# One gated recurrence on one core: products of a level in four PSUM banks at once, chunk states as one chain in tiles of their own

## The chip, the core and the metric

The kernel runs on one core of a Trainium2 chip. A core has a matrix engine (TensorE; PE in the profile, PEld for its weight loads), a vector engine (DVE), a scalar engine (ACT), GpSimd (POOL), a sync engine (SP) that issues DMAs, an on-chip memory with 128 partitions (SBUF) and an accumulator memory for matrix products (PSUM), which the kernel uses as eight banks of 128 x 512 f32. The metric is the device time of one execution in microseconds (us). The kernel before took 2295.3 us, the median of three runs.

## What is computed

One layer of a decoder trunk with 1024 tokens and width 1024: a modulated input, one wide input projection, an HGRN2 gated recurrence (8 heads, 128 x 128 states) beside a retention branch (4 heads), a gated merge, an output projection, a layer norm, and a squared-ReLU MLP. All of it is f32. The change lies in the HGRN2 branch alone. Cut to what matters, for each head:

```python
q = silu(zq);  f = lb + (1 - lb) * sigmoid(zf);  k = (1 - lb) * sigmoid(-zf)
# S_t = diag(f_t) S_{t-1} + k_t^T v_t ,   o_t = q_t S_t      (f_t: one factor per channel)
def step(state, blk):                      # one chunk of tokens
    qc, lfc, kc, vc = blk
    b = cumsum(lfc)                        # log of the running product of f
    scores = einsum('id,ijd,jd->ij', qc, exp(b_i - b_j) where i >= j, kc)
    o = scores @ vc + (qc * exp(b)) @ state
    state = exp(b_last) * state + (kc * exp(b_last - b))^T @ vc
    return state, o
o = o * rsqrt(mean(o*o) + eps) * silu(g)   # per head
```

## The kernel before

**The stage.** `build` runs the eight heads in a loop (lines 1711 to 1715). Each head has two parts, which are Python generators that emit instructions: `h_dense(h)` (line 730), the projections of `q`, `f` and `k` for one head, and `h_rec(p, hd)` (line 770), its recurrence. `weave` (line 89) alternates the emission of `h_dense(h + 1)`, four steps, with the steps of `h_rec` of head `h`. For the last head the four steps are gate projections `gb`. The order of emission is a priority. When the program is built, the framework's scheduler makes one fixed order for each engine out of it: where the next instruction of a higher priority is not ready in the scheduler's own model, a later one that is ready goes ahead. On the chip each engine then runs its fixed order.

**The dense part.** One step of `h_dense` is 24 products of 128x128 by 128x512 into one bank (`dense_T`, line 361; the three calls of `mm3`, lines 175 to 177, because each f32 number is split into two parts). The banks are `psd`, of which there are three (`ps`, line 153). Four steps make 96 products a head. ACT and DVE turn the result into `q`, `f` and `k` (lines 752 to 761) and split the next weights (lines 170 and 171).

**The recurrence.** A head has 1024 tokens in eight chunks of 128. The decay inside a chunk is built by doubling: level 0 pairs neighbouring tokens (lines 781 to 799), and three further levels have the block sizes 2, 8 and 32 (`H_SIZES`, line 802). At each level DVE scales `X` and `k` by products of decays (lines 810, 811 before the products; 831 to 834 after them; the decay products themselves in 813, 814), TensorE makes eight products with 192 columns (line 785 at level 0, line 821 later; an f32 product is two passes in the trace, so 16 passes a level), two to a bank, and DVE takes the wanted entries into the score matrix `S` with predicated copies (lines 788 and 789, or line 828, three for each bank). The banks are `psa`, of which there are two: the third product pair waits until DVE has emptied the first bank. The step before the next level overwrites `k`, so it comes after all products that read `k`.

**The chain of chunks.** Then `k` is turned (`kt`, lines 844 and 846), and for each chunk in turn (lines 848 to 866) there are: `qp` times the state (854) and `S` times `v` (855) into one bank `psc`, an ACT copy of it to `ob` (856), `kt` times `v` (859) into another bank `psc`, and the new state from the old one on DVE (862 for the first chunk, 864 then). There are two `psc` banks and two state tiles `st`. Each four chunks end with a square (868), a sum over it (878, 879), a power on POOL (880), a scaling on ACT (872), a transpose back into bank `psb` (886), a product with the gate `g` (890) and a DMA to DRAM (891). The last three are put off by `H_DEFER` steps with `later` and `tick` (lines 132 to 143). `X`, whose first half is `qp`, exists once, so the first write of the next head to it (line 794) comes after the last product that reads `qp`; `S` has two sets of tiles, by turns.

Of the kernel before, what the change touches and what calls it, by code (L numbers as in the profile page):

```python
# [10 lines left out]
F32 = mybir.dt.float32  # L11
# [3 lines left out]
AF = mybir.ActivationFunctionType  # L15
ALU = mybir.AluOpType
# [3 lines left out]
P = 128  # L20
# [31 lines left out]

H_DEFER = 7

# [70 lines left out]
class Trunk:  # L125
# [644 lines left out]
    def h_rec(self, p, hd):  # L770
        nc = self.nc
        h = 2 * p + hd
        s = self.hst[p][hd]
        q, f, k, v = s["q"], s["f"], s["k"], s["v"]
# [4 lines left out]
        yield  # L779

        for bk in range(4):
            pa = self.ps("a", (P, 384)).rearrange("p (c w b) -> p c w b", c=2, w=3)
            for c in (0, 1):
                n = 2 * bk + c
                nc.tensor.matmul(pa[:, c], k[:, n * P:(n + 1) * P], q[:, :, n * 64:(n + 1) * 64], start=True, stop=True)
            Sv = S[bk // 2][:, bk % 2 * 2:bk % 2 * 2 + 2, :].rearrange("p c (b two) -> p c two b", two=2)
            mk = self.mask8[:, :P].rearrange("p (b two) -> p two b", two=2).unsqueeze(1).to_broadcast([P, 2, 2, 64])
            V.copy_predicated(Sv, mk, pa[:, :, 0:2])
            V.copy_predicated(Sv[:, :, 1], self.mask8[:, P:P + 64].unsqueeze(1).to_broadcast([P, 2, 64]), pa[:, :, 2])
            if bk == 1:  # L790
                yield
        X = self.hX
        qp = X[:, 0]
        V.tensor_tensor(qp.rearrange("p (b two) -> p two b", two=2), q[:, 0::2],
# [3 lines left out]
        Dt = self.hp.tile([P, T // 2], F32, tag="D0", bufs=1, name=self.uid("D"))  # L798
        V.tensor_tensor(Dt, fv[:, 0], fv[:, 1], op=ALU.mult)


        for ln, sz in enumerate(H_SIZES):
# [8 lines left out]
            V.tensor_tensor(Xv[:, 1, 1::2], Xv[:, :, 2], by(Dv[:, 1], 2, B, sz), op=ALU.mult)  # L811
            D2v = D2.rearrange("p (b two) -> p two b", two=2)
            V.tensor_tensor(D2v, Dv[:, 0::2], Dv[:, 1::2], op=ALU.mult)
            V.tensor_tensor(D4, D2v[:, 0], D2v[:, 1], op=ALU.mult)
            yield
            for bk in range(4):
                pa = self.ps("a", (P, 384))
                for c in (0, 1):
                    n = 2 * bk + c
                    mv = X[:, :, n * P:(n + 1) * P].rearrange("p w (b r) -> p b w r", r=4 * sz)[:, :, :, sz:]  # L820
                    nc.tensor.matmul(pa[:, c * 192:(c + 1) * 192].rearrange("p (b w r) -> p b w r", w=2, r=3 * sz),  # L821
                                     k[:, n * P:(n + 1) * P], mv, start=True, stop=True)
                pv = pa.rearrange("p (b w r s) -> p b w r s", w=2, r=3, s=sz)
                Sv = S[bk // 2][:, bk % 2 * 2:bk % 2 * 2 + 2, :].rearrange("p c (b f s) -> p (c b) f s", f=4, s=sz)
                for j, (dst, src) in enumerate(((Sv[:, :, 1::2], pv[:, :, 0, 0::2]), (Sv[:, :, 2:4], pv[:, :, :, 1]),
                                                (Sv[:, :, 2:4], pv[:, :, 1, 0::2]))):
                    o = P + 64 + 384 * ln + 128 * j
                    V.copy_predicated(dst, self.mask8[:, o:o + 128].rearrange("p (b two s) -> p b two s", two=2, s=sz), src)
                if bk == 1:
                    yield  # L830
            V.tensor_tensor(kv[:, 0::2], kv[:, 0::2], Dv[:, 1::2].unsqueeze(3).to_broadcast([P, 2, B, sz]), op=ALU.mult)
            V.tensor_tensor(kv[:, 0:2], kv[:, 0:2], by(D2v[:, 1], 2, B, sz), op=ALU.mult)
            V.tensor_tensor(Xv[:, 0, 1], Xv[:, 0, 1], by(Dv[:, 0], B, sz), op=ALU.mult)
            V.tensor_tensor(Xv[:, 0, 2:4], Xv[:, :, 2], by(D2v[:, 0], 2, B, sz), op=ALU.mult)
            Dt = D4
        yield
        state = None
        for hf in (0, 1):
            g = self.hp.tile([P, 512], F32, tag="g", bufs=3, name=self.uid("g"))
            nc.sync.dma_start(g, self.hg_d[h][:, hf * 512:hf * 512 + 512])  # L840
            pb = self.ps("b")
            for c in range(4):
                cs = slice(hf * 512 + c * P, hf * 512 + c * P + P)
                nc.tensor.transpose(pb[:, c * P:(c + 1) * P], k[:, cs], self.ident)
            kt = self.hp.tile([P, 512], F32, tag="kt", bufs=2, name=self.uid("kt"))
            nc.scalar.activation(kt, pb, AF.Copy)
            ob = self.hp.tile([P, 4, P], F32, tag="ob", bufs=2, name=self.uid("ob"))
            for c in range(4):
                n = 4 * hf + c
                cs = slice(n * P, n * P + P)  # L850
                vn = v[:, n, hd * P:(hd + 1) * P]
                po = self.ps("c", (P, P))
                if n > 0:
                    nc.tensor.matmul(po, qp[:, cs], state, start=True, stop=False)
                nc.tensor.matmul(po, S[hf][:, c, :], vn, start=n == 0, stop=True)
                nc.scalar.activation(ob[:, c, :], po, AF.Copy)
                if n < 7:
                    pu = self.ps("c", (P, P))
                    nc.tensor.matmul(pu, kt[:, c * P:(c + 1) * P], vn, start=True, stop=True)
                    ns = self.hp.tile([P, P], F32, tag="st", bufs=2, name=self.uid("st"))  # L860
                    if n == 0:
                        nc.vector.tensor_copy(ns, pu)
                    else:
                        nc.vector.scalar_tensor_tensor(ns, state, Dt[:, n:n + 1], pu, op0=ALU.mult, op1=ALU.add)
                    state = ns
                yield
# [5 lines left out]
            self.later(3, lambda ob=ob, rs=rs: [nc.scalar.activation(ob[:, c], ob[:, c], AF.Copy, scale=rs[:, c:c + 1]) for c in range(4)])  # L872
            self.later(H_DEFER, lambda ob=ob, hf=hf, g=g: self.h_out(h, hf, ob, g))
            yield
# [709 lines left out]
def build(ctx, tc, ins, out):  # L1584
# [113 lines left out]
    with ExitStack() as s:  # L1698
# [12 lines left out]
        for h in range(HH):  # L1711
            if h + 1 < HH:
                weave(k.h_dense(h + 1), k.h_head_rec(h), 4, 18)
            else:
                weave((next(gb) for _ in range(4)), k.h_head_rec(h), 4, 30)
    k.rst = {}
# [84 lines left out]
```

## Time and profile before

| | us |
|---|---|
| median of three runs (2291.59, 2295.3, 2295.4) | 2295.3 |
| the profiled execution | 2292.25 |
| its span, first to last instruction | 2290.5 |
| DMA busy share in the three windows of one head each | 0.21, 0.17, 0.21 |
| longest wait for a gate `g` or its landing: time to landing | 2.8 to 3.5 |

The recurrence stage runs from about 796 us to about 1133 us of the span: the first product of line 785 starts at 796.0 and the last of line 855 at 1132.6. In the middle of it the heads repeat with a period of about 42 us: the first burst of line 821 of successive heads starts at 888.05, 930.09, 972.12, 1014.15 and 1056.23 us. Matmul rows in the trace overlap (a pass is shown from its start to the modelled end of its pipeline), so the time that a pass really takes is read from start to start, not from its length. In a row such as `961.58 0.89 PE L785 MATMUL ... x4` the first number is the start, the second the time to the end of the last pass of the group, and x4 the number of passes; brackets at the end give idle time before it and what ended it.

### The profile page before, as it was taken

What the parts mean: (1) busy time and instruction counts of PE and PEld (TensorE: products, weight loads), DVE (VectorE), ACT (ScalarE), POOL (GpSimd) and SP (SyncE); (2) the same over time, 40 slices, a digit from 0 to 9 for tenths busy, and PEclk for the clock granted to TensorE, in tenths of its full rate; (3) what the DMA queues carried; (4) which work ended last, traced back from release to release, by engine and by line L of the source; (5) the groups of instructions that cost most, each with busy time, mean ns of one, the idle gap of its engine ahead of it and who ended that gap; (6) DMA issues with size and microseconds to landing.
All of it is one profiled execution on the core that took longest, in us unless ns stands there. A gap on an engine that the chain in (4) does not pass through costs nothing.

```text
span 2290.5 us, 29158 instructions
## 1 busy us (share of the span) xinstructions
PE 2233.6 (98%) x10214; PEld 1818.6 (79%) x10214; DVE 1668.2 (73%) x3024; ACT 981.5 (43%) x1675; POOL 287.5 (13%) x444
## 2 busy tenths in 40 slices
PE   6999999999999999999998999999999999999997
PEld 4888888888888888888866777788888888788886
DVE  7747776467776588888677777877796666767669
ACT  4533344433333333333253334353475555643441
POOL 0111011111111100100112222103111111100001
PEclk9999999999999999999999999999999999999999
DMA  9555543333333411122288878645334444877653
GB/s 304 189 166 166 188 139 115 110 106 112 109 114 108 152 47 65 61 69 79 68 280 259 270 254 284 213 155 203 120 133 171 152 152 152 300 242 243 214 164 129
DMA packets 228563, 375.33 MB, mean 164 GB/s; under 512 B 16584, under 2 KB 126912, under 8 KB 228160
## 3 DMA queue, kind: packets, MB, share of 16 engines
q1 hardware_dynamic: 199664, 279.66, 38.0%
q0 software_dynamic: 28432, 93.35, 10.9%
q8 instruction: 80, 1.31, 0.2%
q14 instruction: 67, 0.55, 0.1%
q10 hardware_dynamic: 320, 0.45, 0.1%
HBM read 275.87 MB, written 97.53 MB: 163 GB/s over the span
## 4 chain that ended last, share of the span: by engine, by line
PE 80%; DVE 7%; DMA 5%; issue 5%; ACT 2%; POOL 1%; SPq 0%; ACTq 0%; DVEq 0%; POOLq 0%
PE psd L176 14%; PE psd L177 14%; PE psd L175 14%; PE psa L176 5%; PE psa L175 5%; PE psa L177 5%; PE psc L175 4%; PE psc L176 3%; PE psc L177 3%; PE psa L821 3%; PE psb L1090 1%; PE psb L175 1%; PE psb L176 1%; PE psb L177 1%; DVE U L171 1%
## 5 line engine op out<-in xcount | busy, mean ns | idle before, releaser
L175 PE MATMUL psd<-U,bh 128*128 128x512 f32 x616 | 239.9, 389 | 0.0
L176 PE MATMUL psd<-U,bh 128*128 128x512 f32 x616 | 239.6, 389 | 0.0
L177 PE MATMUL psd<-U,bl 128*128 128x512 f32 x616 | 239.5, 389 | 0.0
L170 ACT ACTIVATE bh<-s 128x512 fp32r<-128x512 f32 x204 | 128.8, 632 | 249.4 <-PE psd L176 81.3
L171 DVE TENSOR_TENSOR bl<-raw,bh 128x512 fp32r<-128x512 f32 x153 | 104.5, 689 | 144.3 <-ACT bh L170 143.9
L176 PE MATMUL psd<-U,wh 128*128 128x512 f32 x504 | 205.0, 407 | 1.0 <-DVE U L171 0.7
L175 PE MATMUL psd<-U,wh 128*128 128x512 f32 x504 | 203.8, 408 | 1.2 <-ACT U L170 1.0
L177 PE MATMUL psd<-U,wl 128*128 128x512 f32 x504 | 203.5, 404 | 0.0
L171 DVE TENSOR_TENSOR bl<-s,bh 128x512 fp32r<-128x512 f32 x204 | 139.7, 685 | 67.5 <-ACT bh L170 67.4
L170 ACT ACTIVATE bh<-raw 128x512 fp32r<-128x512 f32 x153 | 96.9, 637 | 194.6 <-PE psd L176 99.9
L170 ACT ACTIVATE U<-hr 128x512 fp32r<-128x512 f32 x112 | 70.6, 631 | 153.5 <-issue 73.5
L175 PEld LDWEIGHTS psd<-U,bh 128*128 128x128 f32 x616 | 115.6, 188 | 24.5 <-DVE e L431 0.4
L177 PEld LDWEIGHTS psd<-U,bl 128*128 128x128 f32 x616 | 115.6, 188 | 24.3
L176 PEld LDWEIGHTS psd<-U,bh 128*128 128x128 f32 x616 | 115.6, 188 | 23.8
L175 PE MATMUL psa<-U,bh 128*128 128x512 f32 x312 | 121.4, 389 | 0.0
L176 PE MATMUL psa<-U,bh 128*128 128x512 f32 x312 | 121.4, 389 | 0.0
L177 PE MATMUL psa<-U,bl 128*128 128x512 f32 x312 | 121.4, 389 | 0.0
L176 PEld LDWEIGHTS psd<-U,wh 128*128 128x128 f32 x504 | 96.2, 191 | 21.2 <-DVE U L171 3.6
L175 PEld LDWEIGHTS psd<-U,wh 128*128 128x128 f32 x504 | 95.3, 190 | 20.9 <-ACT U L170 3.7
L177 PEld LDWEIGHTS psd<-U,wl 128*128 128x128 f32 x504 | 96.0, 191 | 17.0 <-issue 0.4
L171 DVE TENSOR_TENSOR U<-hr,U 128x512 fp32r<-128x512 f32 x112 | 76.8, 685 | 41.1 <-ACT U L170 40.9
L170 ACT ACTIVATE wh<-raw 128x512 fp32r<-128x512 f32 (+1 forms) x78 | 52.4, 691 | 120.7 <-PE psd L176 69.1
(430 smaller groups left out, 5667.3 us busy)
## 6 DMA issues: line engine op xcount, KB each, us to landing
raw<-in_w_in SPq DMA_DIRECT2D x126, 512.0 KB, 4.3
raw<-in_w_down SPq DMA_DIRECT2D x48, 512.0 KB, 4.6
raw<-in_w_pb SPq DMA_DIRECT2D x36, 512.0 KB, 4.7
raw<-in_w_ada SPq DMA_DIRECT2D x32, 512.0 KB, 5.5
raw<-in_w_up SPq DMA_DIRECT2D x32, 512.0 KB, 3.6
adw<-in_w_ada SPq DMA_DIRECT2D x16, 512.0 KB, 7.6
rv_d<-e POOLq DMA_DIRECT2D x32, 256.0 KB, 3.1
rg_d<-e POOLq DMA_DIRECT2D x32, 256.0 KB, 2.3
```

Of the source, the lines that this page charges most:

```text
L170: self.nc.scalar.activation(hi, src, AF.Copy)
L171: self.nc.vector.tensor_tensor(lo, src, hi.bitcast(F32), op=ALU.subtract)
L175: r = mm(out, wh, uh, start=start, stop=False, skip_group_check=more)
L176: mm(out, wh, ul, start=False, stop=False, skip_group_check=more)
L177: return r, mm(out, wl, uh, start=False, stop=stop, skip_group_check=more)
L821: nc.tensor.matmul(pa[:, c * 192:(c + 1) * 192].rearrange("p (b w r) -> p b w r", w=2, r=3 * sz), k[:, n * P:(n + 1) * P], mv, start=True, ...
L1090: mm(po, st["q"][:, e, n * P:(n + 1) * P], gs[e], start=False, stop=e == 1)
```

## The change

`H_DEFER` goes from 7 to 4, the weave from 4:18 to 4:13 (and for the last head from 4:30 to 4:18), since the recurrence of a head has 13 steps instead of 19. In `h_rec`:

1. **Levels in bursts.** The eight products of a level go into four banks taken at once, two `psa` and two `psc`. The copies out of the first two banks (`own` at level 0, `put` later) follow in the same step. Those of the last two (`rest`) are emitted after the scaling steps (831 to 834) and after the next level's lines 810 and 811. The decay products `D2`, `D4` move behind the products.
2. **Turning `k`.** Both halves are turned one behind the other, through a `psb` and a `psa` bank, and the two `g` loads follow there.
3. **One chain of states.** All products `kt` times `v` of four (then three) chunks go into one bank, and the seven DVE steps make eight states in tiles of their own (`st` has eight buffers instead of two).
4. **Outputs.** After the states, the outputs of four chunks go into one bank, `S` times `v` first and `qp` times the state second, the groups of a bank kept in turn by `behind`; one ACT copy takes 128x512 instead of four of 128x128. The scaling of `ob` is put off by 2 steps instead of 3.

```diff
-H_DEFER = 7
+H_DEFER = 4
...
+        X = self.hX
+        qp = X[:, 0]
+        Sl = lambda bk: S[bk // 2][:, bk % 2 * 2:bk % 2 * 2 + 2, :]
+        banks = lambda: [self.ps(t, (P, 384)) for t in "aacc"]
+        ps = banks()
         for bk in range(4):
-            pa = self.ps("a", (P, 384)).rearrange("p (c w b) -> p c w b", c=2, w=3)
+            pa = ps[bk].rearrange("p (c w b) -> p c w b", c=2, w=3)
             for c in (0, 1):
                 n = 2 * bk + c
                 nc.tensor.matmul(pa[:, c], k[:, n * P:(n + 1) * P], q[:, :, n * 64:(n + 1) * 64], start=True, stop=True)
-            Sv = S[bk // 2][:, bk % 2 * 2:bk % 2 * 2 + 2, :].rearrange("p c (b two) -> p c two b", two=2)
+
+        def own(bk, pa):
+            pa = pa.rearrange("p (c w b) -> p c w b", c=2, w=3)
+            Sv = Sl(bk).rearrange("p c (b two) -> p c two b", two=2)
...
             V.copy_predicated(Sv, mk, pa[:, :, 0:2])
             V.copy_predicated(Sv[:, :, 1], self.mask8[:, P:P + 64].unsqueeze(1).to_broadcast([P, 2, 64]), pa[:, :, 2])
-            if bk == 1:
-                yield
+
+        own(0, ps[0])
+        own(1, ps[1])
...
+        rest = [lambda bk=bk, ps=ps: own(bk, ps[bk]) for bk in (2, 3)]
...
             V.tensor_tensor(Xv[:, 1, 1::2], Xv[:, :, 2], by(Dv[:, 1], 2, B, sz), op=ALU.mult)
-            D2v = D2.rearrange("p (b two) -> p two b", two=2)
-            V.tensor_tensor(D2v, Dv[:, 0::2], Dv[:, 1::2], op=ALU.mult)
-            V.tensor_tensor(D4, D2v[:, 0], D2v[:, 1], op=ALU.mult)
+            for r in rest:
+                r()
             yield
+            ps = banks()
             for bk in range(4):
-                pa = self.ps("a", (P, 384))
...
+            V.tensor_tensor(D2v, Dv[:, 0::2], Dv[:, 1::2], op=ALU.mult)
+            V.tensor_tensor(D4, D2v[:, 0], D2v[:, 1], op=ALU.mult)
+            put(0, ps[0])
+            put(1, ps[1])
+            yield
...
+            rest = [lambda bk=bk, ps=ps, put=put: put(bk, ps[bk]) for bk in (2, 3)]
             Dt = D4
+        for r in rest:
+            r()
         yield
...
+        kt, g = [], []
+        for hf, tag in ((0, "b"), (1, "a")):
+            pb = self.ps(tag)
...
+            nc.scalar.activation(kt[hf], pb, AF.Copy)
...
+            nc.sync.dma_start(g[hf], self.hg_d[h][:, hf * 512:hf * 512 + 512])
+        yield
+        states = [None]
+        for hf, tag in ((0, "a"), (1, "c")):
+            pu = self.ps(tag)
+            for c in range(4 - hf):
+                nc.tensor.matmul(pu[:, c * P:(c + 1) * P], kt[hf][:, c * P:(c + 1) * P], vn(4 * hf + c), start=True, stop=True)
+            for c in range(4 - hf):
+                n = 4 * hf + c
+                ns = self.hp.tile([P, P], F32, tag="st", bufs=8, name=self.uid("st"))
+                src = pu[:, c * P:(c + 1) * P]
+                if n == 0:
+                    V.tensor_copy(ns, src)
+                else:
+                    V.scalar_tensor_tensor(ns, states[n], Dt[:, n:n + 1], src, op0=ALU.mult, op1=ALU.add)
+                states.append(ns)
+            yield
+        for hf, tag in ((0, "c"), (1, "a")):
+            po = self.ps(tag)
+            prev = None
             for c in range(4):
                 n = 4 * hf + c
+                r = l = nc.tensor.matmul(po[:, c * P:(c + 1) * P], S[hf][:, c, :], vn(n), start=True, stop=n == 0)
+                if prev is not None:
+                    self.behind(r, prev)
                 if n > 0:
+                    l = nc.tensor.matmul(po[:, c * P:(c + 1) * P], qp[:, n * P:n * P + P], states[n], start=False, stop=True)
+                prev = l
+            ob = self.hp.tile([P, 4, P], F32, tag="ob", bufs=2, name=self.uid("ob"))
+            nc.scalar.activation(ob, po.rearrange("p (c e) -> p c e", c=4), AF.Copy)
...
             self.later(1, lambda sq=sq, ms=ms, rs=rs: self.h_factor(sq, ms, rs))
-            self.later(3, lambda ob=ob, rs=rs: [nc.scalar.activation(ob[:, c], ob[:, c], AF.Copy, scale=rs[:, c:c + 1]) for c in range(4)])
-            self.later(H_DEFER, lambda ob=ob, hf=hf, g=g: self.h_out(h, hf, ob, g))
+            self.later(2, lambda ob=ob, rs=rs: [nc.scalar.activation(ob[:, c], ob[:, c], AF.Copy, scale=rs[:, c:c + 1]) for c in range(4)])
+            self.later(H_DEFER, lambda ob=ob, hf=hf: self.h_out(h, hf, ob, g[hf]))
             yield
```

More of the change, by code (lines that the diff above doesn't have):

```diff
@@ L789, in h_rec @@
             V.copy_predicated(Sv[:, :, 1], self.mask8[:, P:P + 64].unsqueeze(1).to_broadcast([P, 2, 64]), pa[:, :, 2])
-            if bk == 1:
-                yield
-        X = self.hX
-        qp = X[:, 0]
+        own(0, ps[0])
+        own(1, ps[1])
         V.tensor_tensor(qp.rearrange("p (b two) -> p two b", two=2), q[:, 0::2],
@@ L820, in h_rec, with put @@
                     mv = X[:, :, n * P:(n + 1) * P].rearrange("p w (b r) -> p b w r", r=4 * sz)[:, :, :, sz:]
-                    nc.tensor.matmul(pa[:, c * 192:(c + 1) * 192].rearrange("p (b w r) -> p b w r", w=2, r=3 * sz),
+                    nc.tensor.matmul(ps[bk][:, c * 192:(c + 1) * 192].rearrange("p (b w r) -> p b w r", w=2, r=3 * sz),
                                      k[:, n * P:(n + 1) * P], mv, start=True, stop=True)
+            def put(bk, pa, ln=ln, sz=sz):
                 pv = pa.rearrange("p (b w r s) -> p b w r s", w=2, r=3, s=sz)
-                Sv = S[bk // 2][:, bk % 2 * 2:bk % 2 * 2 + 2, :].rearrange("p c (b f s) -> p (c b) f s", f=4, s=sz)
+                Sv = Sl(bk).rearrange("p c (b f s) -> p (c b) f s", f=4, s=sz)
                 for j, (dst, src) in enumerate(((Sv[:, :, 1::2], pv[:, :, 0, 0::2]), (Sv[:, :, 2:4], pv[:, :, :, 1]),
@@ L828, in h_rec @@
                     V.copy_predicated(dst, self.mask8[:, o:o + 128].rearrange("p (b two s) -> p b two s", two=2, s=sz), src)
-                if bk == 1:
-                    yield
+            D2v = D2.rearrange("p (b two) -> p two b", two=2)
+            V.tensor_tensor(D2v, Dv[:, 0::2], Dv[:, 1::2], op=ALU.mult)
[3 more added lines that the diff above has]
+            yield
             V.tensor_tensor(kv[:, 0::2], kv[:, 0::2], Dv[:, 1::2].unsqueeze(3).to_broadcast([P, 2, B, sz]), op=ALU.mult)
@@ L834, in h_rec @@
             V.tensor_tensor(Xv[:, 0, 2:4], Xv[:, :, 2], by(D2v[:, 0], 2, B, sz), op=ALU.mult)
+            rest = [lambda bk=bk, ps=ps, put=put: put(bk, ps[bk]) for bk in (2, 3)]
             Dt = D4
+        for r in rest:
+            r()
         yield
[L837 to L841, printed above, removed]
+        kt, g = [], []
+        for hf, tag in ((0, "b"), (1, "a")):
+            pb = self.ps(tag)
             for c in range(4):
@@ L844, in h_rec @@
                 nc.tensor.transpose(pb[:, c * P:(c + 1) * P], k[:, cs], self.ident)
-            kt = self.hp.tile([P, 512], F32, tag="kt", bufs=2, name=self.uid("kt"))
-            nc.scalar.activation(kt, pb, AF.Copy)
-            ob = self.hp.tile([P, 4, P], F32, tag="ob", bufs=2, name=self.uid("ob"))
+            kt.append(self.hp.tile([P, 512], F32, tag="kt", bufs=2, name=self.uid("kt")))
+            nc.scalar.activation(kt[hf], pb, AF.Copy)
+            g.append(self.hp.tile([P, 512], F32, tag="g", bufs=3, name=self.uid("g")))
@@ new lines, in h_rec @@
+            nc.sync.dma_start(g[hf], self.hg_d[h][:, hf * 512:hf * 512 + 512])
+        yield
+        vn = lambda n: v[:, n, hd * P:(hd + 1) * P]
+        states = [None]
[13 more added lines that the diff above has]
+            yield
@@ L853, in h_rec @@
                 if n > 0:
[L854 to L865, printed above, removed]
@@ L866, in h_rec @@
-                yield
+                    l = nc.tensor.matmul(po[:, c * P:(c + 1) * P], qp[:, n * P:n * P + P], states[n], start=False, stop=True)
+                prev = l
+            ob = self.hp.tile([P, 4, P], F32, tag="ob", bufs=2, name=self.uid("ob"))
+            nc.scalar.activation(ob, po.rearrange("p (c e) -> p c e", c=4), AF.Copy)
             sq = self.hp.tile([P, 512], F32, tag="ot", bufs=2, name=self.uid("sq")).rearrange("p (c e) -> p c e", c=4)
@@ L1712, in build @@
             if h + 1 < HH:
-                weave(k.h_dense(h + 1), k.h_head_rec(h), 4, 18)
+                weave(k.h_dense(h + 1), k.h_head_rec(h), 4, 13)
             else:
-                weave((next(gb) for _ in range(4)), k.h_head_rec(h), 4, 30)
+                weave((next(gb) for _ in range(4)), k.h_head_rec(h), 4, 18)
     k.rst = {}
```

3 lines of the change are left out of this document (removed).

## The prediction

> **What bounds the kernel now.** I read the page first, then the stretches of one head each in the recurrence stage, then the groups of the same stretch, and last the order of time on PE.
>
> ```profile
> span 2290.5 us, 29158 instructions
> PE 2233.6 (98%) x10214; PEld 1818.6 (79%) x10214; DVE 1668.2 (73%) x3024; ACT 981.5 (43%) x1675; POOL 287.5 (13%) x444
> PEclk9999999999999999999999999999999999999999
> ```
>
> PE is busy nearly everywhere and its clock is never lowered, so time is won only where PE stands still, or spends longer on a pass than the pass needs. The stage itself, three heads of the eight:
>
> ```profile
> core 0: us, PE busy (x) PEld busy (x) DVE busy (x) ACT busy (x) POOL busy (x), PEclk, DMA share, GB/s
> 930.09:972.12 42.03, 41.34 (x222) 34.39 (x221) 35.59 (x91) 15.06 (x34) 3.37 (x5) 1.00 0.21 69
> 972.12:1014.15 42.03, 41.31 (x220) 34.39 (x221) 35.58 (x91) 15.06 (x34) 3.37 (x5) 1.00 0.17 57
> 1014.15:1056.23 42.08, 41.36 (x220) 34.40 (x221) 35.58 (x91) 15.07 (x34) 3.37 (x5) 1.00 0.21 70
> ```
>
> A head takes 42.05 us. DVE is busy 35.6 of them and idle 6.5; ACT (15), POOL (3) and DMA (a share of 0.2) are far off. PE shows 41.3, but its rows overlap, so I count what its passes need, from start to start:
>
> ```profile
> 784.69 0.39 PE L176 MATMUL psd<-U,wh 128*128 128x512 f32 x1
> ...
> 795.79 0.39 PE L177 MATMUL psd<-U,wl 128*128 128x512 f32 x1
> 796.02 1.46 PE L785 MATMUL psa<-hq,k 128*128 128x192 f32 x8
> 797.18 0.53 PE L175 MATMUL psd<-U,wh 128*128 128x512 f32 x1
> 797.55 0.40 PE L176 MATMUL psd<-U,wh 128*128 128x512 f32 x1
> ...
> 806.23 1.54 PE L821 MATMUL psa<-U,k 128*128 128x192 f32 x8
> 807.48 0.53 PE L177 MATMUL psd<-U,wl 128*128 128x512 f32 x1
> 807.84 0.40 PE L175 MATMUL psd<-U,wh 128*128 128x512 f32 x1
> ...
> 954.88 0.60 PE L844 MATMUL psb<-cst,k 128*128 128x128 f32 x4
> 955.23 0.47 PE L176 MATMUL psd<-U,wh 128*128 128x512 f32 x1
> ```
>
> Between 784.69 and 795.79 lie 49 dense passes: 11.10/49 = 0.227 us each. The eight passes of line 785 and one dense pass take 797.55 - 796.02 = 1.53, so a recurrence pass takes (1.53 - 0.227)/8 = 0.163. Four transposes take 0.35, 0.088 each. A pass of the chain (lines 854, 855, 859) takes 0.11, as 964.19 - 963.97 = 0.22 for two shows below. One head needs 96 dense passes, 64 recurrence passes (four levels of 16), 44 chain passes (16 + 14 + 14) and 16 transposes: 21.8 + 10.4 + 4.8 + 1.4 = 38.4 us. So **3.6 us of a head's 42.05 are not work of PE**. Where they are:
>
> ```profile
> 960.81 0.48 PE L175 MATMUL psd<-U,wh 128*128 128x512 f32 x1
> 961.58 0.89 PE L785 MATMUL psa<-hq,k 128*128 128x192 f32 x4 [0.30 <-DVE U L789]
> 962.31 0.39 PE L854 MATMUL psc<-st,U 128*128 128x128 f32 x2
> 962.53 0.39 PE L855 MATMUL psc<-U,U 128*128 128x128 f32 x2
> 962.75 0.39 PE L859 MATMUL psc<-U,kt 128*128 128x128 f32 x2
> 962.98 0.82 PE L785 MATMUL psa<-hq,k 128*128 128x192 f32 x4
> 963.67 0.46 PE L854 MATMUL psc<-st,U 128*128 128x128 f32 x2
> 963.97 0.39 PE L855 MATMUL psc<-U,U 128*128 128x128 f32 x2
> 964.19 0.39 PE L859 MATMUL psc<-U,kt 128*128 128x128 f32 x2
> 964.97 0.91 PE L886 MATMUL psb<-cst,ob 128*128 128x128 f32 x3 [0.39 <-ACT ob L872]
> 965.63 0.48 PE L176 MATMUL psd<-U,wh 128*128 128x512 f32 x1
> ```
>
> From 960.81 to 965.63 are 4.82 us, and the passes in it need 0.23 + 8 x 0.163 + 12 x 0.11 + 3 x 0.088 = 3.1. This one spell loses 1.7 us: 0.54 ahead of line 785, whose `psa` bank DVE has not emptied, 0.56 ahead of the transposes 886, which wait for the scaling, 0.4 inside those, the rest at seams. The other 1.9 us are spread over some fourteen visits of PE to other shapes between dense passes, 0.14 each. A clean visit costs less: at 806.23 eight passes take 807.84 - 806.23 - 0.227 = 1.38 instead of 1.30, a seam of 0.08.
>
> What DVE waits for, over the same three heads:
>
> ```profile
> L828 DVE COPY_PREDICATED U<-mask,psa 128x128 f32<-128x128 uint8 x108 | 29.7, 313 | 8.4 <-PE psa L821 6.9
> L788 DVE COPY_PREDICATED U<-mask,psa 128x256 f32<-128x256 uint8 x12 | 8.5, 731 | 0.0
> L789 DVE COPY_PREDICATED U<-mask,psa 128x128 f32<-128x128 uint8 x12 | 4.9, 458 | 0.0
> L864 DVE SCALAR_TENSOR_TENSOR st<-st,D,psc 128x128 f32<-128x128 f32 x18 | 6.1, 338 | 5.0 <-PE psc L859 4.8
> L794 DVE TENSOR_TENSOR U<-hq,f 128x1024 f32<-128x1024 f32 x3 | 3.7, 1226 | 1.3 <-PE psc L854 1.3
> ```
>
> Per head 2.8 us ahead of the copies of line 828 and 1.7 ahead of the state steps. Head after head is one serial line through DVE and the recurrence passes, but dense passes fill PE meanwhile. I therefore hold PE for the bound, with DVE and its waits (42.05) pulling level, and price the change by PE's 3.6 us.
>
> **The change part by part.** No pass of PE, no copy and no multiplication of DVE goes away; ACT's output copies alone get fewer. So the floor of 38.4 us stays, and the change can win 8 x 3.6 = 29 us at the very most.
>
> *Bursts.* Lines 785 and 821 now reach PE as 16 passes into four banks. Before, the trace groups a level as 8 + 4 + 4, nine visits for the three levels of line 821. With bank pairs freed in one go, I expect one or two visits a level. That saves 3 to 6 visits, at 0.08 (clean) to 0.14 (mean): 0.24 to 0.84 us. I take five at 0.11, **-0.55**. The copies for banks 2 and 3 go behind line 811, six at 29.7/108 = 0.275, so DVE has 1.65 us to do before the new level's first copies, and PE needs 4 x 0.163 = 0.65 for a bank; DVE's 2.8 us of waiting there should nearly go. That is worth nothing by itself as long as PE is the bound. The cover is thin in one place: bank 2 of the burst must be free 1.3 us after the burst begins and bank 3 1.95 us after; the copies free them 0.8 and 1.65 us after line 811. If PE stands there 0.3 us a level, 0.9 us a head go back.
>
> *Turning `k` and the loads of `g`.* The eight transposes and two ACT copies stay. The two `g` loads are issued together on SP, later than the first was; they are used only in line 890, several steps on, so nobody waits: 0. With three `g` buffers, SP would wait for the previous head's line 890, put off by four steps of thirteen, which is over by then.
>
> *The chain.* Now seven state steps follow each other on DVE, 7 x 0.34 = 2.4 us, behind one ACT copy and the products of one bank.
>
> ```profile
> 956.23 0.42 PE L859 MATMUL psc<-U,kt 128*128 128x128 f32 x2
> ...
> 968.20 0.47 PE L175 MATMUL psd<-U,wh 128*128 128x512 f32 x1
> ```
>
> What took the 12 us between these two rows, the first product of the chain and the dense pass behind its last, becomes about 0.35 + 0.6 + 0.9 + 2.4 + 0.5 = 5 us. PE no longer swaps between the chain and line 785, so the wait of 0.54 and the seams of the spell above (0.2 of them) should go: **-0.75**. The waits for the scaling I leave as they are: the square, sum, power and scaling are the same, and the put-off of four steps covers about as much work as seven shorter steps did.
>
> *New waits.* The next head's level 0 needs banks that the chain holds. The trace of before has no such wait. Its bounds: 0, if dense passes fill it, and 0.22 + 0.6 for the last product and the copy of 128x512, if none do; it can't be below 0, since no such wait existed to be removed. Nearest is the line 785 wait above, 0.30 shown on PE with dense passes running out. I take **+0.2**. Queued behind a waiting product on PE is everything, dense passes included.
>
> *Outputs.* One ACT copy of 128x512 replaces four of 128x128. ACT has 27 us of slack a head: 0. `behind` fixes an order that the products have anyway.
>
> The Trainium skill, PSUM — Partial Sum Buffer, section on bank collisions, says that two engines may not touch one bank at the same time, even at different columns, and that users must be kept apart by whole banks. The kernel before gives one product or one finished sum to a `psc` bank, so no row here shows it either way; by it the first state step would wait for all four products of its bank, and the sum would come out as in the third rival.
>
> Sum: -0.55 - 0.75 + 0.2 = **-1.1 us a head, 8 heads: -8.8 us**, the last head like the others, since gate projections fill PE there. The profiled execution took 2292.25 us, so it would take 2283.5. It lies 3 us below the median of the runs shown; from that the sum gives 2286.5. I name 2285, between the two.
>
> **The rivals.**
>
> *All but the seams go.* Nothing waits, and some thirteen visits at 0.08 remain: 1.0 of the 3.6 us. That is -2.6 a head, -21 us, 2274 from the median. For it speaks that the chain's ping-pong is the only large loss. Against it: rows such as line 886's wait come from POOL and ACT, which the change doesn't speed up. Chance 0.18.
>
> *DVE's line becomes the bound: slower.* Before, DVE had the next head's copies 788 and 789, (8.5 + 4.9)/3 = 4.5 us, to do in the gaps of the chain. Now the four banks are in the chain's hands, and these copies come after it. DVE's idle time would be 6.5 - 2.8 - 1.0 (of line 864's) = 2.7, plus up to 4.5 = 7.2, and 35.6 + 7.2 = 42.8, 0.75 more than now: +6 us, 2301 from the median; with 0.22 more for the next state product, 2303. It decides from the point where DVE idles more than 6.5 us a head. For it: `X` and the banks leave few ways to overlap heads. Against: DVE has lines 833, 834 and six copies (2.7 us) for the chain's start. Chance 0.20.
>
> *The hand-over eats it: no change.* If the state steps wait for whole banks, three further products (0.66) and two (0.44) stand in the chain. That is 1.1 us a head and 8.8 in all, just the gain: 2295 from the median. The same result comes if PE's order puts the losses elsewhere, as 0.3 us at three levels would. Chance 0.17, of which 0.07 for the whole-bank wait. The Trainium skill's section named above (PSUM — Partial Sum Buffer, bank collisions) would demand that wait.
>
> **How the numbers follow.** The forecast has 0.45, from 2279 to 2290. A difference of 0.2% (4.6 us) is about what a measurement of this kernel can tell from no change. Forecast and first rival lie below that by more: 0.45 + 0.18, less 0.01 for the forecast's edge, is faster 0.62; same 0.17 + 0.01 = 0.18; slower 0.20. The range that leaves out a tenth on either side is from 2272 (first rival, bounds of the burst included) to 2303.
>
> **What would show it.** Right: the heads' period falls from 42.05 to 41 us or less; line 821 appears in groups of 8 to 16 passes; the idle time ahead of 828 and 864 falls under 2 us a head; no 785 among 854 to 859. Wrong: DVE idles over 6.5 us a head while PE stands still ahead of 785 (second rival); the first state step starts only after the fourth product of its bank and the period stays (third); line 886 waits longer than 1 us a head for the scaling.

## The result and the profile after

The changed kernel takes **2277.25 us** (median of six runs, 2273.12 to 2278.7) against 2294.73 (six runs, 2289.16 to 2295.93): a ratio of **0.9924, 95% interval 0.9911 to 0.9937**, 17.5 us less. Its profiled execution took 2276.54 us, 15.7 less than that of before. From the page:

```profile
span 2274.7 us, 29056 instructions
PE 2216.5 (97%) x10214; PEld 1824.2 (80%) x10214; DVE 1661.5 (73%) x3024; ACT 969.2 (43%) x1627; POOL 289.1 (13%) x444
PEclk9999999999999999999999999999999999999999
```

The number of passes is the same. The page alone doesn't say where 16 us went. Three heads of the changed kernel, in the view of windows (time, busy time with instructions for each engine, clock, DMA share, GB/s):

```profile
923.16:964.31 41.15, 39.50 (x221) 34.85 (x221) 34.08 (x92) 13.59 (x28) 3.82 (x4) 1.00 0.24 77
...
1005.46:1046.62 41.16, 39.51 (x221) 34.85 (x221) 34.07 (x92) 13.59 (x28) 3.83 (x4) 1.00 0.28 87
```

The period went from 42.05 to 41.15 us: 0.9 a head, 7.2 for eight. More than half of the 17.5 us is not there. To find the rest I add up PE's passes along its rows from 785 us on, at the prediction's prices for a pass (0.227, 0.163, 0.11 and 0.088 us), and call "lost" what the time in the trace has beyond that work. Two shapes of the retention stage have prices of their own: 128x512 on plain f32 operands (line 1090 of before) takes 0.428 us from start to start throughout, 128x256 about 0.26. The last products of the last head come at about 310 us of work; from there to 520 us of work the retention stage runs. Other prices within a few thousandths of a us shift single figures by about 1 us, much the same in all runs.

| lost time, us | before | after | difference |
|---|---|---|---|
| heads (to 310 us of work) | 26.2 | 19.7 | 6.5 |
| retention stage (310 to 520) | 28.5 | 19.4 | 9.1 |
| of this between 380 and 400 | 10.4 | 1.6 | 8.8 |

**The larger part lies in a stage whose code the change doesn't touch.** Two readings follow, one for each place.

*In the heads.* PE's timeline of the changed kernel, first around a level, then at the chain:

```profile
917.66 1.46 PE L793 MATMUL psa<-hq,k 128*128 128x192 f32 x8
918.96 1.46 PE L793 MATMUL psc<-hq,k 128*128 128x192 f32 x8
920.26 0.60 PE L917 MATMUL psb<-cst,ob 128*128 128x128 f32 x4
...
923.16 1.57 PE L831 MATMUL psa<-U,k 128*128 128x192 f32 x8 [1.60 <-DVE k L807]
924.57 1.46 PE L831 MATMUL psc<-U,k 128*128 128x192 f32 x8
...
944.90 1.16 PE L874 MATMUL psa<-U,kt 128*128 128x128 f32 x8
945.81 0.48 PE L175 MATMUL psd<-U,wh 128*128 128x512 f32 x1
...
949.33 0.83 PE L874 MATMUL psc<-U,kt 128*128 128x128 f32 x6
950.00 0.61 PE L890 MATMUL psc<-U,U 128*128 128x128 f32 x4
...
953.12 0.39 PE L894 MATMUL psa<-st,U 128*128 128x128 f32 x2
953.26 0.48 PE L175 MATMUL psd<-U,wh 128*128 128x512 f32 x1
```

(Lines 793 and 831 are 785 and 821 of before, 807 is 797; 874, 890 and 894 are the chain's 859, 855 and 854; 917 is 886.) A level is one visit of 16 passes, with nothing between its banks. The chain's last 36 passes follow each other without another shape between them, 949.33 to 953.26: 3.93 us, 0.109 each, with no loss. But ahead of the first burst of line 831 there is a wait of **1.60 us** that the kernel before did not have. DVE's timeline shows what line 807 was behind:

```profile
919.55 0.69 DVE L761 TENSOR_TENSOR hq<-psd,sg 128x512 f32<-128x512 f32 x1 [2.05 <-ACT sg L759]
920.15 1.30 DVE L799 COPY_PREDICATED U<-mask,psa 128x256 f32<-128x256 uint8 x2
921.26 0.77 DVE L800 COPY_PREDICATED U<-mask,psa 128x128 f32<-128x128 uint8 x2
921.83 0.77 DVE L799 COPY_PREDICATED U<-mask,psc 128x256 f32<-128x256 uint8 x1
922.39 0.72 DVE L807 TENSOR_TENSOR k<-k,f 128x512 f32<-128x512 f32 x1
```

Line 761 of the next head's dense part, for which DVE stands idle for 2.05 us, and five copies (799, 800) come first; only then is `k` scaled for the next burst. PE has by then run out of dense passes that its order allows.

*In the retention stage.* Its first loads, `v <- rv_d` on SP, go into memory that the heads' tiles held, so SP waits for the last output DMA of head 7. First the kernel before, from the views of POOL, SP's waits (total, times, longest) and SP's timeline:

```profile
1140.07 0.60 POOL L891 DMA_DIRECT2D oh_d<-ot  x1 [2.88 <-DVE ot L890]
...
SPq L1050 <- DMA oh_d<-ot: 40.1, 1, 40.1
...
1143.17 0.81 SPq L1050 DMA_DIRECT2D v<-rv_d  x2
...
1210.72 2.89 SPq L313 DMA_DIRECT2D raw<-in_w_pa  x2
```

Then the same of the changed kernel:

```profile
1120.24 0.54 POOL L922 DMA_DIRECT2D oh_d<-ot  x1 [0.45 <-DVE ot L921]
...
SPq L1081 <- DMA oh_d<-ot: 15.3, 1, 15.3
...
1123.15 0.81 SPq L1081 DMA_DIRECT2D v<-rv_d  x2
...
1188.36 0.38 SPq L313 DMA_DIRECT2D raw<-in_w_pa  x1
```

The last output leaves 20 us earlier, the `v` load is issued 20 us earlier, and SP comes to the third load of the weights `w_pa` 22 us earlier. What the late weights cost before stands in its ACT, DVE and PE timelines:

```profile
1220.37 1.15 ACT L170 ACTIVATE wh<-raw 128x512 fp32r<-128x512 f32 x2 [5.35 <-DMA raw<-in_w_pa]
...
1221.03 2.07 DVE L171 TENSOR_TENSOR wl<-raw,wh 128x512 fp32r<-128x512 f32 x3 [5.83 <-ACT wh L170]
1223.02 0.68 DVE L1035 TENSOR_TENSOR t<-psa,cst 128x512 f32<-128x512 f32 x1
...
1223.76 1.01 PE L1133 MATMUL psa<-acc,small 128*1 128x256 f32 x2 [5.45 <-DVE t L1035]
1224.70 0.80 PE L176 MATMUL psd<-U,wh 128*128 128x512 f32 x1
...
1225.72 0.63 PE L175 MATMUL psd<-U,wh 128*128 128x512 f32 x1
1226.15 0.63 PE L176 MATMUL psd<-U,wh 128*128 128x512 f32 x1
```

ACT and, in its in-order queue, DVE wait for the weights; line 1035, which needs none, is queued behind line 171; PE stands still for 5.45 us. Afterwards, until 1227.9, the dense passes start 0.43 us apart (1225.72 to 1226.15) instead of 0.227: PE's clock is at half (the last section has the rows). That loses 2.3 us more (worked out in the table of the runs below), so that stall and slow passes come to 5.45 + 2.3 = 7.7 us, of 8.8 in the table's last row. The changed kernel has no such stall: between 1203 and 1223 us its PE is busy 20.00 of 20.00.

### The profile page after: what moved, and what is told of

Its sections match the earlier page's. It is cut to its first block, busy times and chain, and to the rows that moved or that the text cites. A ratio compares the mean times of both kernels' runs of the same rounds, so it can differ in the third digit from the quotient of the medians.

```text
span 2274.7 us, 29056 instructions
## 1 busy us (share of the span) xinstructions
PE 2216.5 (97%) x10214; PEld 1824.2 (80%) x10214; DVE 1661.5 (73%) x3024; ACT 969.2 (43%) x1627; POOL 289.1 (13%) x444
## 3 DMA queue, kind: packets, MB, share of 16 engines
q1 hardware_dynamic: 199664, 279.66, 38.7%
## 4 chain that ended last, share of the span: by engine, by line
PE 82%; DVE 8%; issue 5%; DMA 3%; ACT 2%; POOL 1%; SPq 0%; ACTq 0%; DVEq 0%; POOLq 0%
PE psd L175 14%; PE psd L176 14%; PE psd L177 14%; PE psa L176 5%; PE psa L177 5%; PE psa L175 5%; PE psc L175 4%; PE psc L177 4%; PE psc L176 4%; PE psb L1121 2%; PE psc L1113 2%; PE psb L175 2%; PE psb L176 2%; PE psb L177 1%; PE psa L831 1%
## 5 line engine op out<-in xcount | busy, mean ns | idle before, releaser
L175 PE MATMUL psd<-U,wh 128*128 128x512 f32 x504 | 203.9, 407 | 0.3 <-ACT U L170 0.3
L176 PE MATMUL psd<-U,wh 128*128 128x512 f32 x504 | 198.9, 395 | 1.0 <-DVE U L171 0.7
```

The costliest lines, as they stand in the source:

```text
L175: r = mm(out, wh, uh, start=start, stop=False, skip_group_check=more)
L176: mm(out, wh, ul, start=False, stop=False, skip_group_check=more)
```

## The experiments

The theory: A, that the earlier output of the last head is worth some 9 us in the retention stage, through the time at which its loads start. The rival B: that the time comes from the heads, and the stage behind them only shifts. `lost` below is as in the table above, with its prices in all runs; the lag is the time from the end of 310 us of PE work to the first `v` load. "Half clock" is the time in the retention stage for which the trace has a granted clock of 0.50; behind it stands the PE work that was done in that time, and as much time again was lost, since every pass took about twice as long. All this is of the one profiled execution of each run.

| run | median us | ratio and interval | lost in heads | in retention | half clock: us, lost by it | lag of the load |
|---|---|---|---|---|---|---|
| before (first profile) | 2294.73 | | 26.2 | 28.5 | 6.8, 2.3 | 21.8 |
| e0_before | 2295.33 (one run) | | 26.3 | 30.6 | 6.8, 2.6 | 23.6 |
| after | 2277.25 | 0.9924 [0.9911, 0.9937] | 19.7 | 19.4 | 0 | 8.3 |
| a_again | 2281.77 | 0.9945 [0.993, 0.9961] | 22.3 | 22.7 | 10.2, 4.2 | 7.2 |
| e1_late_tail | 2284.35 | 0.9954 [0.9937, 0.9972] | 19.7 | 31.3 | 13.7, 6.6 | 19.0 |
| e7_delay2 | 2276.92 | 0.9931 [0.9915, 0.9946] | 19.8 | 20.4 | 0 | 13.0 |
| e2_last_chain | 2287.85 | 0.9974 [0.9958, 0.9989] | 26.3 | 22.4 | 0 | 16.3 |
| e3_levels | 2286.52 | 0.9957 [0.994, 0.9974] | 26.8 | 21.2 | 3.4, 1.9 | 12.5 |
| e4_chain | 2286.58 | 0.996 [0.9942, 0.9978] | 21.8 | 28.1 | 10.2, 4.7 | 14.7 |
| e5_first | 2279.23 | 0.9937 [0.9912, 0.9961] | 20.9 | 19.0 | 3.4, 1.5 | 10.6 |
| e6_half | 2273.06 | 0.9917 [0.9902, 0.9932] | 15.8 | 22.5 | 10.2, 4.9 | 7.9 |
| e8_half5 (e6 again) | 2276.43 | 0.9933 [0.9919, 0.9946] | 16.0 | 23.4 | 10.2, 4.6 | 9.5 |
| e9_quarter | 2270.95 | 0.9907 [0.9894, 0.9921] | 14.8 | 22.0 | 6.8, 3.1 | 7.1 |

Ratios are to the kernel before on the same chip: 2294.29 us for e1 to e4, 2292.47 for e5 to e7, 2293.31 for a_again, e8 and e9.

### The last output late, in the changed kernel: e1 and e7

The output DMA of the last half head is repeated on SP, with the same data to the same place; `v` must wait for the repeats. Five repeats are e1, two are e7.

```diff
         nc.gpsimd.dma_start(self.oh_d[h][:, hf * 512:hf * 512 + 512], ot)
+        if h == HH - 1 and hf == 1:
+            for _ in range(5):
+                nc.sync.dma_start(self.oh_d[h][:, hf * 512:hf * 512 + 512], ot)
```

> The changed kernel, but the last write of the last head to DRAM is repeated five times on SP, each repeat behind the one before, so that the loads of the retention stage, which reuse that memory, start some 12 us later; the heads are untouched. Theory A (the time won outside the heads comes from the retention loads, which start at 1123 us instead of 1143 us): the late loads bring back a stall of PE in the retention stage, 2283 to 2288 us. Theory B (the order of the retention instructions is what differs, the start of the loads does not matter): within 3 us of the changed kernel, 2274 to 2280 us.

2284.35 us, in A's band and outside B's. The heads keep their gain (lost 19.7), the retention stage loses 31.3, no less than in the kernel before, and the same stall is back, in SP's, ACT's and PE's timelines of e1:

```profile
1134.00 0.80 SPq L1084 DMA_DIRECT2D v<-rv_d  x2
...
1209.61 1.15 ACT L170 ACTIVATE wh<-raw 128x512 fp32r<-128x512 f32 x2 [4.80 <-DMA raw<-in_w_pa]
...
1212.22 1.01 PE L1167 MATMUL psa<-acc,small 128*1 128x256 f32 x2 [4.43 <-DVE t L1069]
...
1213.76 0.63 PE L177 MATMUL psd<-U,wl 128*128 128x512 f32 x1
1214.18 0.63 PE L175 MATMUL psd<-U,wh 128*128 128x512 f32 x1
```

Line 1167 is 1133 of before. The passes run at the same slow pace behind it (0.42 us from 1213.76 to 1214.18). By the medians a delay of 11 us of one load costs 2284.35 - 2277.25 = 7.1 us; beside the second measurement of the changed kernel (a_again, 2281.77) it would be 2.6, so the size is better read from the trace: 4.43 us of stall and some 1.7 behind it at half clock, 6 us. The other 10.2 us at half clock, from 1280.39 and 1317.94 us on, begin at gaps of 2.31 and 2.87 us that the changed kernel has too, at 2.85 and 1.21 us and without the half clock; whether the late load brought them is not shown.

> The changed kernel with the last write repeated twice instead of five times, so that the retention loads start some 5 us later than in the changed kernel. If the loss in the retention stage grows in step with the delay: 2279 to 2281 us. If it is one stall that appears only beyond some delay: 2275 to 2278 us.

With two repeats the load comes at 1128.01, 5 us later than in the changed kernel, and the time is as without that delay: 2276.92. So the price does not grow in step with the delay; between 5 and 11 us it has a step.

### The chain for the last head alone, in the kernel before: e2

```diff
+        if h == HH - 1:
+            yield from self.h_chain(p, hd, h, S, k, v, qp, Dt)
+            return
         state = None
...
-                weave((next(gb) for _ in range(4)), k.h_head_rec(h), 4, 30)
+                weave((next(gb) for _ in range(4)), k.h_head_rec(h), 4, 19)
```

`h_chain` holds the new turning of `k`, chain and outputs; `st` gets eight buffers.

> The kernel before, with the new chain (and its outputs and put-offs) for the last head alone; heads 0 to 6 keep the old levels and the old chain. Theory A: the last head's tail ends some 8 to 10 us earlier, the retention loads start that much earlier, and PE's stall of 5.5 us with the half clock behind it goes: 2283 to 2288 us. Theory B: only the last head's own part of the gain, 1 us: 2292 to 2295 us.

2287.85 us, in A's band: 6.4 us below its 2294.29, with the heads losing as much as before (26.3). In its profile the load is issued at 1137.76, 5.4 us earlier than before, and that is enough: there is no stall ahead of the passes that are line 1133 in the kernel before, and no half clock (22.4 lost). But this profile is of the fastest of ten executions (2282.42 us at a mean granted clock of 0.997); three of the ten took 2293.52 to 2295.77 us, as long as the kernel before, at 0.993 to 0.995, and none of those was profiled. With e1, A is supported from both sides: by e1 in time and trace, by e2 in the median and in one trace.

### Each half of the change alone: e3 and e4

e3 is the kernel before with the new levels and the old chain; e4 is the changed kernel with the old levels (two `psa` banks) and the new chain. Core of e3:

```diff
+        banks = lambda: [self.ps(t, (P, 384)) for t in "aacc"]
...
+        ps = banks()
...
-            pa = self.ps("a", (P, 384)).rearrange("p (c w b) -> p c w b", c=2, w=3)
+            pa = ps[bk].rearrange("p (c w b) -> p c w b", c=2, w=3)
...
+        rest = [lambda bk=bk, ps=ps: own(bk, ps[bk]) for bk in (2, 3)]
```

> The kernel before with the new levels alone (16 passes into four banks), the old chain of chunks in all heads. If the levels carry the gain of the heads: a period of 41.2 us a head or less, 7 us in all, 2286 to 2289 us. If the chain carries it: a period of 41.6 to 42.2 us, because each chunk of the old chain still makes PE visit other shapes, 2290 to 2296 us. Either way the last head's tail ends late and the stall in the retention stage stays.

2286.52 us, but by neither branch. The period is 41.93 and the heads lose 26.8: **the levels alone win next to nothing there.** The load came at 1134.48, 8.7 us earlier than before, and the retention stage lost only 21.2. That "either way the stall stays" was wrong. Where the levels' gain in the heads went shows PE's timeline of e3 at the old chain:

```profile
959.29 0.49 PE L879 MATMUL psc<-U,kt 128*128 128x128 f32 x2 [1.12 <-ACT ob L876]
```

The old chain hands its two `psc` banks to and fro, and PE waits 1.12 us in one place for ACT's copy out of one.

> The kernel before with the new chain alone (states in own tiles, outputs of four chunks in a bank, H_DEFER 4), the old levels through two banks. If the chain carries the gain: a period of 41.2 us or less and an early end of the last head's tail, 2276 to 2280 us, as the whole change. If the levels carry the gain of the heads: a period of 41.7 to 42.2 us, and only the retention stage's part is won, 2283 to 2288 us.

The period is 41.25 (the first dense pass behind a burst of level 0 starts at 919.45, 960.71 and 1001.96 us), the heads lose 21.8: the chain carries 4.4 of the 6.5 us. The time, 2286.58, is in the band of the other branch all the same, since the retention stage lost 28.1, 8.7 more than in the changed kernel, though the lag is only 14.7. The trace has two stalls there, of 3.38 us at 1147.5 and of 3.34 us at 1204.9. The second stands again behind a wait for `w_pa`: ACT is idle for 3.36 us for it. Behind both PE runs at half clock, which loses 4.7 us more; the changed kernel's profile has the first gap too (3.64 us), but no half clock behind it.

### The new wait: e5 and e6

e5 emits the first two steps of a head's recurrence ahead of the next head's dense part, so that line 807 comes ahead of line 761 on DVE:

```diff
+            rec = k.h_head_rec(h)
+            next(rec)
+            next(rec)
...
-                weave(k.h_dense(h + 1), k.h_head_rec(h), 4, 13)
+                weave(k.h_dense(h + 1), rec, 4, 11)
...
-                weave((next(gb) for _ in range(4)), k.h_head_rec(h), 4, 18)
+                weave((next(gb) for _ in range(4)), rec, 4, 16)
```

> The changed kernel with the first two steps of a head's recurrence (the level 0 burst among them) emitted ahead of the next head's dense steps, so that dense passes stand behind that burst and not before it. In the changed kernel PE stands 1.6 us a head ahead of the first burst of line 831, waiting for DVE's line 807. If that wait is the last large loss of PE and dense passes can cover it, it goes, but PE then waits up to 0.9 us for ACT's copy of the outputs ahead of level 0: a period of 40.3 to 40.7 us, 2270 to 2274 us. If DVE's line is the bound by now, the wait only moves: a period of 41 us or more, 2275 to 2279 us.

2279.23, and the period stays at 41.15 to 41.2: the wait moved, though not to the place that I named, but to the transposes, which wait for ACT's scaling, in PE's timeline of e5:

```profile
919.76 0.62 PE L917 MATMUL psb<-cst,ob 128*128 128x128 f32 x2 [1.27 <-ACT ob L903]
```

e6 does the same, but keeps half of a dense step, 12 products, ahead of it, so that PE has passes at both places:

```diff
-            pd = self.dense_T(wh, wl, hf)
+            pd = self.ps("d")
+            for kk in range(KT):
+                if kk == 4 and what == "hq" and hf == 0:
+                    yield
+                uh, ul = self.ublk(kk, hf)
+                self.mm3(pd, wh[:, kk], wl[:, kk], uh, ul, kk == 0, kk == KT - 1)
...
-                weave(k.h_dense(h + 1), k.h_head_rec(h), 4, 13)
+                dense, rec = k.h_dense(h + 1), k.h_head_rec(h)
+                next(dense)
+                next(rec)
+                next(rec)
+                weave(dense, rec, 4, 11)
```

> As the run before, but with half a dense step (12 passes) ahead of the level 0 burst and half behind it, so that both waits have dense passes to cover them. If PE is the bound: both waits go, a period of 39.6 us (floor 38.4 and some twelve seams), 2265 to 2269 us. If DVE's line is the bound: a period of 40.8 us or more, 2273 to 2278 us.

2273.06 us, the period 40.52. From the view of windows of e6:

```profile
919.13:959.65 40.52, 39.91 (x221) 34.77 (x220) 34.19 (x93) 13.65 (x28) 3.17 (x4) 1.00 0.23 79
```

The period falls by 0.63; the wait of 1.60 us ahead of the first burst is gone, and one of some 0.6 a head is left, ahead of the second, for line 827 on DVE (822 of the changed kernel).

### Again, and a version that beats both: e0, a_again, e8, e9

> The kernel before, profiled a second time. If its stall of PE ahead of line 1133 in the retention stage belongs to the kernel, it is there again, 4 us or longer, with the half clock behind it; if it was an accident of one execution, PE stands there less than 1 us.

2295.33 us; the stall ahead of line 1133 is there again with 5.00 us, and so is the slow pace behind it.

> The changed kernel again, beside the next two on the same chip: 2274 to 2279 us.

2281.77 (2275.42 to 2283.72), above what I expected: its profile has a stall of 5.09 us at 1147 us, ahead of line 1061, where the first profile has 3.64, and PE is at half clock for 10.2 us of the retention stage and 3.4 us of the heads, where the first profile is at full clock. Without the 4.2 us lost by it, its retention stage loses 18.5, as much as in the first profile (19.4). The changed kernel was thus measured at 0.9924 and 0.9945; both intervals lie below 1.

> The kernel of the run with half a dense step ahead of the level 0 burst, timed in more rounds beside the changed kernel. If its shorter heads (40.5 us instead of 41.15) reach the end: 3 to 5 us below the changed kernel. If the retention stage takes them back: within 2 us of it.

2276.43, 5.3 us below a_again on the same chip, but 3.4 above e6, the same kernel: about as much as the changed kernel's two measurements differ (4.5). The runs of e8 and a_again overlap.

e9 gives 6 products ahead and 18 behind (`kk == 2`), and `H_DEFER = 5`, so that the scaling has one step more:

```diff
-H_DEFER = 4
+H_DEFER = 5
...
+                if kk == 2 and what == "hq" and hf == 0:
+                    yield
```

> As the run before, with 6 dense passes ahead of the level 0 burst and 18 behind it, and H_DEFER 5, so that the transposes of the outputs come after the next burst. If PE's waits in the heads can be covered by dense passes: the wait of 0.6 us ahead of level 2 and the rest go, a period of 39.7 to 40.1 us, 3 to 5 us below the run before. If the serial line through DVE sets the period by now: a wait moves to the next burst, the period stays at 40.4 to 40.7 us and the time within 2 us.

**2270.95 us** (2269.66 to 2274.12), no run of it above any of a_again (2275.42 the lowest): faster than the changed kernel and than the kernel before, on the same chip. The period is 40.30, between the two expectations; the wait moved once more, in PE's timeline of e9:

```profile
921.00 0.39 PE L176 MATMUL psd<-U,wh 128*128 128x512 f32 x1
922.11 0.63 PE L922 MATMUL psb<-cst,ob 128*128 128x128 f32 x4 [0.72 <-DVE ot L926]
```

Here the transposes wait for a `psb` bank that DVE's product with `g` (line 926) has yet to empty. How much of the 5.5 us between e8 and e9 is scatter, the runs don't settle.

## Why the prediction was right, and where not

The direction held, and 2277.25 lies 8 us below the 2285 named, in the range, below the forecast's own 2279 to 2290 (the second measurement, 2281.77, lies within). In part that is luck: the heads gave less than forecast, and a place that the prediction didn't look at gave more than the heads.

- **PE as the bound: right.** The period followed PE's losses. DVE's idle time, 41.15 - 34.08 = 7.1 us a head, went over the 6.5 from which the second rival was to decide, and the period fell. That rival took DVE's busy time of 35.6 as fixed and added the waits to it; the busy time fell too, to 34.08 (why is not shown), and most of the idle time lies beside PE's work. The forecast's own sign, a period of 41 us or less, was just missed.
- **"Its clock is never lowered": wrong.** The page's 9 stands for 0.9 and more of a slice of 57 us. In the heads the clock is at 1.00, but the kernel before runs at 0.50 from 1221.07 to 1227.90 us, in the retention stage, and there lay the larger gain.
- **The floor of 38.4 is a little low.** Four transposes were priced by 955.23 - 954.88 = 0.35 us, but the dense pass behind them takes 0.31 (to 955.54) instead of 0.227, so that they cost 0.43, 0.11 each. The floor is then 38.7, and 3.3 of the 42.05 us are not work.
- **The chain, -0.75: right.** The period of e4 is 42.05 - 41.25 = 0.8 lower; by lost time it is 4.4/8 = 0.55. The spell's loss is gone: 36 passes in 3.93 us. The time from the chain's first product to the dense pass behind its last went from 12.0 to 8.4 us (944.90 to 953.26), not to 5, since 15 dense passes stand in it; on PE that costs nothing.
- **Bursts, -0.55: mis-sized, as were the new waits, +0.2.** Together they come to 41.15 - 41.25 = -0.1 beside the new chain and to as much alone (e3), instead of -0.35. The wait is 1.6 us, and not where I put it: not for a bank that the chain holds, but for `k`, which DVE scales behind the copies of level 0 and line 761. Without it the bursts would stand at -0.1 - 1.6 = -1.7 at most, three times my term; e6, which has one of 0.6 in its place, brings 0.63 of that. I had counted "1.65 us to do before the new level's first copies" and asked only whether DVE would starve. What stands in front of PE's next *operand* I had not asked.
- **DVE's waiting ahead of the copies should nearly go: right**, and worth nothing by itself, as said. From the groups of the changed kernel, 780 to 1150 us:

```profile
L840 DVE COPY_PREDICATED U<-mask,psc 128x128 f32<-128x128 uint8 x144 | 41.1, 312 | 0.7
L840 DVE COPY_PREDICATED U<-mask,psa 128x128 f32<-128x128 uint8 x144 | 35.4, 318 | 1.8 <-PE psa L831 1.6
L880 DVE COPY st<-psa 128x128 f32<-128x128 f32 x8 | 2.3, 292 | 11.6 <-PE psa L874 11.6
```

- **The hand-over by whole banks (third rival): its wait came, its price did not.** Line 880 starts at 946.09, behind all four products of its bank (944.90 to 945.81), after 1.67 us of idle time on DVE; in all 11.6 us over eight heads. PE has 15 dense passes to do between 945.81 and 949.33, and loses nothing. That is how the Trainium skill, PSUM — Partial Sum Buffer, section on bank collisions, wants users kept apart; the trace agrees.
- **Outputs and loads of `g` at 0: right in the heads.** ACT's busy time fell from 15.06 to 13.6 a head, and line 921 has no idle time ahead of it in the stretch of three heads.
- **The sum, -1.1 a head and -8.8 in all:** the period says -0.9 and -7.2, the lost time -6.5.
- **The step that failed: "the last head like the others".** For PE it was. But the last head's final DMA also opens the memory for the next stage's first loads, and it came 20 us earlier: 6.5 us of it because the heads lose less, the rest (the lag, 21.8 to 8.3) because the last product of the last head stands earlier in PE's order, behind 307 us of work instead of 320. From there to the DMA it takes no less than before (1111.39 to 1120.24 us, 8.9; before 1132.48 to 1140.07, 7.6). Each half of the change brings about half of that step: with the new levels alone there are 313 us of work ahead of the last product (e3), with the new chain alone 314 (e4). The prediction followed no queue past the end of the heads. That left out 9 us in the retention stage: with that DMA late, e1 has the 4.43 us of stall and the slow passes behind it again, and e2 brings 6.4 with the last head alone.
- **The first rival ("all but the seams go", 2274)** came nearer with its number than the forecast (by the first measurement, not by the second), for another reason: of the 3.6 us a head that it started from, 41.15 - 38.4 = 2.75 are still lost, not 1.0.

The lag sorts the runs only roughly: at 19 us and over the retention stage loses 28.5 to 31.3 us, at 17 and under 19.0 to 28.1. Without what the half clock took it sorts them fully, 24.7 to 28.0 against 17.4 to 23.4. So what a_again lost beyond the changed kernel there (3.3) is the half clock, and of e4's 8.7 it is 4.7; most of e4's rest is the stall of 3.34 us for `w_pa`. What is open: why the same gap ahead of line 1061 is 3.64 us long in one execution of the changed kernel and 5.09 in another.

## What to carry to other kernels

When the end of a stage moves, follow its last DMA into the next one: memory that is used again ties the next stage's loads to it, and a late load can meet an in-order queue far behind, where it holds up work that doesn't need it. A stall that is filled on one engine often moves to the next operand in line (here from `k` to the scaling to a bank); what helps is to leave passes for both places, as e6 and e9 do, not to move them all to one. Count the work of the bounding engine and compare lost time stage by stage, with the granted clock beside it, before a gain is put down to the lines that changed.

## What the hardware showed beside that

**A stall on PE can cost more than itself.** Behind 5.45 us without a pass (before), and behind 5.00 and 4.43 (e0, e1), the dense passes took 0.43 us or so instead of 0.227 for a while. The view of windows of the kernel before has the granted clock, third from the right, and PE's busy time, behind the comma:

```profile
1217.66:1221.07 3.41, 0.65 (x5) 0.34 (x3) 0.04 (x1) 0.70 (x2) 0.00 (x0) 1.00 0.67 248
1221.07:1224.49 3.42, 0.73 (x2) 0.09 (x2) 3.33 (x6) 3.19 (x7) 0.00 (x0) 0.50 0.49 155
1224.49:1227.90 3.41, 3.41 (x9) 2.52 (x9) 2.76 (x8) 0.60 (x1) 1.42 (x3) 0.50 1.01 386
```

A shorter gap sometimes does the same. The first timeline below is of e6, the second of the changed kernel, at the same sixteen passes:

```profile
1139.93 3.79 PE L1066 MATMUL psa<-U,U 128*128 128x128 f32 x16 [3.43 <-DVE U L171]
1143.37 0.77 PE L175 MATMUL psd<-U,wh 128*128 128x512 f32 x1
```

```profile
1144.44 2.05 PE L1061 MATMUL psa<-U,U 128*128 128x128 f32 x16 [3.64 <-DVE U L171]
1146.25 0.48 PE L175 MATMUL psd<-U,wh 128*128 128x512 f32 x1
```

They took 1143.37 - 1139.93 = 3.44 us in the one and 1.81 in the other, though the gap in the second is the longer. The Trainium skill, TensorE: Matmul & The Clock Gate, section "HAM oscillation — how this bites in real kernels", asks for no idle gaps of PE over some 3.4 us. The four gaps of 3.43 to 5.45 us agree with it, the gap of 3.64 does not, and neither does one of 2.31 us (e1, at 1280.0) with half clock behind it: the length alone does not decide.

What decides shows when the traces are laid out in time. In all thirteen the granted clock is 1.00 or 0.50, and it changes only at the bounds of windows of 3.41 us that follow each other without a break, as in the rows above (from 1227.90 it is 1.00 again). Counted from 100 us on, there are 24 windows at full clock in which PE's rows cover 0.43 of the window or less, and every one is followed by a window at half clock; of the 8178 with more than 0.46 none is; of the five between, one. From half clock, the 25 windows with 0.89 or more lead back to full clock, the 8 with less than 0.76 to another one at half. The gap of 3.43 us in e6 lies mostly in one window, which keeps 0.95 us of PE's time (0.28); the gap of 3.64 us is shared by two, which keep 1.51 and 1.68 us (0.44 and 0.49):

```profile
1135.55:1138.96 3.41, 0.95 (x5) 0.43 (x3) 2.13 (x2) 2.75 (x5) 0.16 (x1) 1.00 0.79 309
```

```profile
1139.29:1142.71 3.42, 1.51 (x7) 0.90 (x5) 1.37 (x2) 2.29 (x3) 0.00 (x0) 1.00 0.69 253
1142.71:1146.12 3.41, 1.68 (x15) 1.68 (x16) 3.41 (x5) 3.23 (x6) 0.54 (x1) 1.00 0.68 213
```

So the same gap can cost up to 1.7 us more for each window at half clock, or nothing, by where it falls.

**The price of a late load has a step in it.** Five us more cost nothing that could be measured (e7), eleven some 6 (e1).
